# Neighbourhood values as float32 products, two heads side by side, and modulation weights in their own ring

## The chip, the cores and the metric

The kernel runs on one core of one Trainium2 chip. The metric is the device time of one execution in microseconds (us); lower is better.

## The reference

One step of a small transformer with two layers, on 512 latent tokens (a grid of 8 rows by 64 columns) and 128 prompt tokens, model width 1024, all in float32. Layer 0 mixes tokens by neighbourhood attention with 16 heads of 64; layer 1 by grouped-query attention with rotary positions. Each layer ends in a gated feed-forward part with a width-3 convolution. Scales, shifts and gates of both layers come from small products of the conditioning vectors with `ada_w`. The change is in layer 0, whose mixer is:

```python
q, k, v = split(h @ w_qkv)                       # 16 heads of 64
s_lat = einsum('brqhd,brkwhd->bhrqkw', qg, kg) * scale     # 8 rows x 16 columns around each query
s_lat = where(col_ok, s_lat + bias, -inf)
s_ctx = einsum('brqhd,bchd->bhrqc', qg, k_ctx) * scale     # 128 cached keys
p = softmax(concat([s_lat, s_ctx]))
o = einsum(p_lat, vg) + einsum(p_ctx, v_ctx)     # the value products
```

The prompt tokens attend only to each other. A modulation is `silu(c) @ ada_w + ada_b`, cut into six rows of 1024 for each layer.

## The kernel before

Tokens are 640 columns: 512 latent, 128 prompt. The NA stage (neighbourhood attention of layer 0, `with l_na`, from line 714) works head by head. `TensorE` follows an order written out by hand: every matmul depends on the one before it in program order (`pe`, line 97). The other engines' instructions stand in an order that a scheduler made when the kernel was built, and each engine takes them in that order.

**Splits.** Large products are made of float32r parts: a weight `raw` is loaded into the ring `wr` of the pool `wp` (4 buffers), ACT casts it to `wh`, POOL or DVE subtracts to get `wl` (`wsplit`, line 150), and three matmuls (high by high, low by high, high by low) go into one accumulation (`passes`, line 166).

**A head.** For each of 16 heads, `Head.scores(slot)` (line 874) makes the scores of one of four blocks of 128 queries: two matmuls `s`, a DVE step that adds the bias and takes the extreme, the exponential on ACT (`p`), a reciprocal on DVE, a multiplication on POOL. `Head.turns(i)` (line 894) transposes four 128x128 blocks of `p` into a PSUM bank `tp`, and `split_turned` (line 640) makes two parts of them: ACT casts to `th`, DVE subtracts to `tl`. `Head.values(i)` (line 903) multiplies both with the values. The value tile `vt` holds for each head 64 high columns and 64 low columns side by side, so that one matmul with 128 weight columns gives both halves: rows 0 to 63 of the bank `po` hold the high part, rows 64 to 127 the low part. `Head.out` (line 919) copies the two halves on ACT into `ot` tiles, and after the odd head of a pair `pair_out` (line 925) adds them on POOL into `of0`, which holds a pair of heads on 128 partitions. The prompt's attention (steps `p0`, `p1`, `p2`, once in four heads) does the same with `prompt_turn`, `prompt_out`.

**The order.** `ORDER` (line 46) is the list of a head's steps, and `ORDER2` that of heads 13 to 15. `t0` to `t2` are the transposes of this head, `s0` to `s3` the scores of the next, `v0` to `v2` the value products, `p0` to `p2` the prompt's. `f` takes the next step of `stream` (line 951), which runs through the query, key and value projections of later heads (`qk` and `vp`, 8 matmul groups each; their weights are loaded one item ahead), and after head 12 the first output products `y`. `a` takes the next step of `ada_work` (line 246), the modulation rows: a row of `ada_w` (128x1024) is loaded into `wr` of `wp`, and some steps later four matmuls `ada` of 32 weight columns use it as their moving operand. So projection weights and modulation weights take turns in one ring of four buffers (line 968).

**After head 12** the output weights are split (`m0.weights`, pinned in program order), `of0` is split into `oh` and `ol` (`o_split`, line 931), and the output products start.

Of the kernel before, what the change touches and what calls it, by code (L numbers as in the profile page):

```python
# [18 lines left out]
P = 128  # L19
D = 1024  # L20
KC = D // P
NS = 512
# [16 lines left out]
NPT = 6  # L39
TH = 322  # L40
# [5 lines left out]
ORDER = "a f a f p0 t0 a s0 f s1 t1 a f v0 t2 a a f a v1 f p1 f a a s2 a s3 v2 f f f a a p2 f f".split()  # L46
ORDER2 = "t0 p0 s0 s1 f a f a f f t1 v0 t2 a a f a f f a a p1 v1 s2 a f a s3 f v2 f p2 a f f".split()
# [44 lines left out]
def hybrid_step(ctx: ExitStack, tc: tile.TileContext, A, O):  # L92
# [330 lines left out]
    def na_v_tiles():  # L423
        return [vpool.tile([P, 6, 2, 2, HD], F32R, tag="vt", name="vt") for _ in range(2)]

    def na_v_put(vts, c, src):
        s4 = src.rearrange("p (a d) -> p a d", a=4)
        for i, vt in enumerate(vts):
            hi = vt[:, c, :, 0, :]
            nc.scalar.copy(hi, s4[:, 2 * i : 2 * i + 2, :])  # L430
            nc.vector.tensor_sub(vt[:, c, :, 1, :], s4[:, 2 * i : 2 * i + 2, :], f32(hi))
# [16 lines left out]
    with ExitStack() as s:  # L448
# [107 lines left out]
        vts_of[0] = na_v_tiles()  # L556
# [83 lines left out]
    def split_turned(ap, tp, n=512, nb=2):  # L640
        th = ap.tile([P, 512], F32R, tag="th", name="th", bufs=nb)
        tl = ap.tile([P, 512], F32R, tag="tl", name="tl", bufs=nb)
        nc.scalar.copy(th[:, 0:n], tp[:, 0:n])
        nc.vector.tensor_sub(tl[:, 0:n], tp[:, 0:n], f32(th[:, 0:n]))
        bk.put(tp)
        return th, tl

    def prompt_turn(ap, pp, nb=2):
# [3 lines left out]
        return split_turned(ap, tp, nb=nb)  # L652

    def prompt_out(ap, po, dsts):

        ta = ap.tile([P, 2, P], F32, tag="ta", name="ta", bufs=1)
        tb = ap.tile([P, 2, P], F32, tag="tb2", name="tb2", bufs=1)
        p4 = po.rearrange("p (a b c) -> p a b c", a=2, b=2)
        for b in range(2):
            own, _ = own_oth(b)  # L660
            nc.scalar.copy(ta[own], p4[0:64, :, b, :])
            nc.scalar.copy(tb[own], p4[64:128, :, b, :])
        bk.put(po)
        for j, dst in enumerate(dsts):
            nc.gpsimd.tensor_add(dst, ta[:, j, :], tb[:, j, :])
# [48 lines left out]
    with l_na:  # L714
# [12 lines left out]
        def na_v_items(g):  # L727
            d = {}

            def load():  # L730
                d["w"] = [wsplit(rows(wqkv, 4 * i, 4, 2048 + 256 * g, 256), 4, 256, nc.gpsimd) for i in range(2)]
                d["v"] = na_v_tiles()
# [122 lines left out]
        class Head:  # L855
# [38 lines left out]
            def turns(self, i):  # L894
# [6 lines left out]
                self.t[i] = split_turned(ap, tp)  # L901

            def values(self, i):
                b = self.b
                vt = vts_of[self.h // 4][(self.h // 2) % 2]
                if i == 0:
                    self.po = bk.get("po")
                po = self.po
                if i == 0:
                    for n, x in enumerate(self.t[i]):  # L910
                        mm(po, vt[:, 5, b, :, :], x, start=n == 0, stop=False)
                    return
                for a, c in enumerate(self.BANKS[i]):
                    ov = po[:, c * P : c * P + 256] if c < 3 else po.rearrange("p (a b) -> p a b", b=P)[:, 0::3, :]
                    for n, x in enumerate(self.t[i]):
                        mm(ov, vt[:, c, b, :, :], x[:, a * 256 : a * 256 + 256], start=False,
                           stop=c == 3 and n == 1)

            def out(self, tabs):
                own, _ = own_oth(self.b)  # L920
                nc.scalar.copy(tabs[0][own], self.po[0:64, :])
                nc.scalar.copy(tabs[1][own], self.po[64:128, :])
                bk.put(self.po)

        def pair_out(p, tabs):
            om = of0[p][:, 0:NS].rearrange("p (r c) -> p r c", c=GW)
# [41 lines left out]
        ada0 = ada_work(l_na.enter_context(pool("ada")), wp, 3, 2, ((0, 2), (0, 4), (0, 3)))  # L968
# [13 lines left out]
        tabs = None  # L982
        for h in range(H):
            nxt = Head(h + 1) if h + 1 < H else None
            if h % 2 == 0:
                tabs = [ap.tile([P, 512], F32, tag=f"ot{i}", name=f"ot{i}", bufs=1) for i in range(2)]
            g = h // 4
            pr = h % 4 == 1
            order = ORDER if h < 13 else ORDER2
            for i, step in enumerate(order):  # L990
# [9 lines left out]
                elif step[0] == "v":  # L1000
                    head.values(int(step[1]))
                if step == "v2":
                    head.out(tabs)
                    if h % 2:
                        pair_out(h // 2, tabs)
# [7 lines left out]
                if pr and step == "p1":  # L1013
                    pth = prompt_turn(ap, pp)
                if pr and step == "p2":
                    po = bk.get("po")
                    for j in range(4):
                        vt = vts_of[g][j // 2]
                        for n, x in enumerate(pth):
                            mm(po[:, j * P : j * P + P], vt[:, 4, j % 2, :, :], x[:, j * P : j * P + P],  # L1020
                               start=n == 0, stop=n == 1)
                    prompt_out(ap, po, [of0[2 * g + j][:, NS:T] for j in range(2)])
# [512 lines left out]
    def gqa_prompt(g):  # L1535
# [11 lines left out]
        def two():  # L1547
            tp = bk.get("tp")
            for i in range(4):
                turn(tp[:, i * P : i * P + P], d["pp"][:, i, :], ident)  # L1550
            x = d["t"] = d["pool"].tile([P, 4, P], F32, tag="ptp", name="ptp", bufs=1)
            nc.scalar.copy(x, tp.rearrange("p (a b) -> p a b", a=4))
            bk.put(tp)
# [270 lines left out]
```

## Time and profile before

| what | us |
|---|---|
| median of three runs (lowest to highest) | 1701.52 (1698.48 to 1703.72) |
| the profiled execution | 1699.22 |
| its span in the trace | 1697.4 |
| NA stage: heads 0 to 12, and the rest to the output products | 95 to 334, 334 to 395 |
| TensorE busy in the span | 94% |
| DVE, ACT, POOL busy in the span | 61%, 53%, 44% |

A row of the trace reads: start, duration, engine, line of the kernel, operation, tile written <- tiles read, shape. PE is TensorE's matmul, PEld its weight load, DVE VectorE, ACT ScalarE, POOL GpSimd; SPq is the queue of SyncE, which issues the large loads. A matmul's duration holds its way through the array, so that what it costs in a sequence is read from the start of the next one. The granted clock is the share of TensorE's clock that it was given.

### The profile page before, as it was taken

The numbers are of one execution on the slowest core, as the hardware profiler recorded it, in microseconds if no ns is written. First come the engines' busy times: TensorE is split into PE (matmuls) and PEld (weight loads), VectorE is DVE, ScalarE is ACT, GpSimd is POOL, SyncE is SP. The second block draws the span as 40 slices with busy tenths as digits, with TensorE's granted clock in tenths as the row PEclk, the third lists the DMA queues.
The fourth block names the chain that finished last, engine by engine and source line by source line (L and its number), as shares of the span: only waits on it lengthen the run. The fifth ranks groups of instructions, "written<-read, shape, count | busy, mean of one in ns | idle before, by whom it ended". The sixth has DMA issues, their size and how long they took to land.

```text
span 1697.4 us, 26300 instructions
## 1 busy us (share of the span) xinstructions
PE 1589.7 (94%) x9709; PEld 1376.1 (81%) x9709; DVE 1039.7 (61%) x1725; ACT 903.6 (53%) x1721; POOL 751.7 (44%) x651
## 2 busy tenths in 40 slices
PE   6899998999999899989979888999998999998998
PEld 3788897977988788988868666777887999997876
DVE  4444454557875555672375776775696788784264
ACT  5466657655554444553355444664555665663353
POOL 3544545444245354442344345442424555652253
PEclk9999999989999999999989998999999999999999
DMA  9544544116376576347557410001636333336574
GB/s 269 150 112 121 141 127 118 32 63 224 113 235 203 189 218 185 121 153 236 161 187 232 133 38 13 2 1 63 211 112 188 115 120 98 117 117 212 174 238 170
DMA packets 193220, 242.43 MB, mean 143 GB/s; under 512 B 11108, under 2 KB 149572, under 8 KB 193092
## 3 DMA queue, kind: packets, MB, share of 16 engines
q1 hardware_dynamic: 182232, 233.13, 43.7%
q10 hardware_dynamic: 10860, 7.62, 2.3%
q8 instruction: 76, 1.25, 0.3%
q14 instruction: 52, 0.43, 0.1%
HBM read 214.38 MB, written 26.34 MB: 142 GB/s over the span
## 4 chain that ended last, share of the span: by engine, by line
PE 58%; DVE 13%; DMA 8%; POOL 7%; ACT 6%; issue 6%; ACTq 1%; SPq 0%; POOLq 0%; DVEq 0%
PE acc L104 17%; PE ux L104 10%; PE y L104 5%; PE uz L104 4%; PE po L104 3%; PE s L104 3%; DMA wr<-in_ada_w 3%; PE tp L107 3%; PE qk L104 3%; PE uy L104 3%; PE vp L104 3%; DMA wr<-in_na_w_qkv 2%; POOL wl L1117 2%; DVE t L1193 2%; PE ada L104 2%
## 5 line engine op out<-in xcount | busy, mean ns | idle before, releaser
L157 POOL TENSOR_TENSOR wl<-wr,wh 128x1024 fp32r<-128x1024 f32 x80 | 196.3, 2457 | 279.6 <-ACT wh L155 274.9
L1117 POOL TENSOR_TENSOR wl<-wr,wh 128x1024 fp32r<-128x1024 f32 x80 | 194.7, 2451 | 68.7 <-ACT wh L1116 59.3
L104 PE MATMUL ux<-B,wh 128*128 128x322 f32 x832 | 201.9, 313 | 1.9 <-DVE B L210 1.8
L1193 DVE SCALAR_TENSOR_TENSOR t<-C,cw,t 128x644 f32<-128x644 f32 x176 | 156.6, 890 | 55.8 <-ACT t L1191 54.9
L104 PE MATMUL acc<-wh,alo 128*128 128x512 f32 x440 | 175.5, 399 | 10.7 <-DVE alo L1086 10.7
L104 PE MATMUL acc<-wh,ahi 128*128 128x512 f32 x440 | 175.6, 399 | 9.5 <-DVE act L1204 9.5
L155 ACT CAST wh<-wr 128x1024 fp32r<-128x1024 f32 x148 | 153.5, 1047 | 45.0 <-DMA wr<-in_na_w_qkv 17.5
L104 PE MATMUL acc<-wl,ahi 128*128 128x512 f32 x440 | 174.7, 397 | 0.0
L104 PE MATMUL uz<-B,wh 128*128 128x322 f32 x640 | 158.4, 315 | 0.0
L104 PEld LDWEIGHTS ux<-B,wh 128*128 128x128 f32 x832 | 143.6, 189 | 9.6 <-issue 3.3
L1086 DVE TENSOR_TENSOR alo<-ain,ahi 128x384 fp32r<-128x384 f32 (+1 forms) x88 | 55.1, 631 | 141.8 <-ACT ahi L1084 141.8
L104 PE MATMUL ux<-B,wl 128*128 128x322 f32 x416 | 129.2, 311 | 0.0
L1084 ACT CAST ahi<-ain 128x384 fp32r<-128x384 f32 (+1 forms) x88 | 40.5, 462 | 166.3 <-PE acc L104 139.8
L104 PE MATMUL qk<-hT,wh 128*128 128x384 f32 (+1 forms) x512 | 126.6, 320 | 0.4 <-DVE qs L799 0.4
L104 PEld LDWEIGHTS uz<-B,wh 128*128 128x128 f32 x640 | 111.6, 190 | 6.6 <-issue 3.7
L1117 POOL TENSOR_TENSOR vl<-wr,vh 128x1024 fp32r<-128x1024 f32 x38 | 96.5, 2540 | 34.2 <-ACT vh L1116 34.2
L104 PEld LDWEIGHTS acc<-wh,alo 128*128 128x128 f32 x440 | 84.4, 192 | 30.4 <-DVE alo L1086 11.9
L1116 ACT CAST wh<-wr 128x1024 fp32r<-128x1024 f32 x88 | 89.5, 1049 | 35.0 <-DVE wr L1140 33.6
L104 PEld LDWEIGHTS acc<-wh,ahi 128*128 128x128 f32 x440 | 84.6, 192 | 28.4 <-issue 10.2
L1191 ACT ACTIVATE t<-C,cw 128x644 f32<-128x644 f32 x88 | 78.7, 894 | 50.7 <-DVE C L1221 47.4
L157 DVE TENSOR_TENSOR wl<-wr,wh 128x1024 fp32r<-128x1024 f32 x68 | 91.1, 1353 | 21.5 <-ACT wh L155 21.0
L104 PE MATMUL uz<-B,wl 128*128 128x322 f32 x320 | 100.0, 313 | 0.5 <-POOL wl L1117 0.4
(264 smaller groups left out, 4193.8 us busy)
## 6 DMA issues: line engine op xcount, KB each, us to landing
wr<-in_ada_w SPq DMA_DIRECT2D x88, 512.0 KB
wr<-in_ffn_w_up SPq DMA_DIRECT2D x88, 512.0 KB
wr<-in_ffn_w_down SPq DMA_DIRECT2D x88, 512.0 KB
act<-act SPq DMA_DIRECT2D x44, 321.0 KB
wr<-in_na_w_qkv SPq DMA_DIRECT2D x24, 512.0 KB
mod<-modrow SPq DMA_DIRECT2D x20, 512.0 KB
ain<-act SPq DMA_DIRECT2D x44, 192.0 KB
xres<-xo SPq DMA_DIRECT2D x15, 512.0 KB
```

Source lines behind the costliest of these rows:

```text
L104: pe(nc.tensor.matmul(*a, **k))
L107: pe(nc.tensor.transpose(*a, **k))
L155: i = nc.scalar.copy(hi, raw)
L157: j = (low or nc.vector).tensor_sub(lo, raw, f32(hi))
L1084: nc.scalar.copy(hi[:, 0 : c1 - c0], ain[:, 0 : c1 - c0])
L1086: nc.vector.tensor_sub(lo[:, 0 : c1 - c0], ain[:, 0 : c1 - c0], f32(hi[:, 0 : c1 - c0]))
L1116: nc.scalar.copy(hl[0], src)
L1117: low.tensor_sub(hl[1], src, f32(hl[0]))
L1191: nc.scalar.activation(t, taps(0), AF.Identity, bias=cw[:, 3, n : n + 1], scale=cw[:, 1, n : n + 1])
L1193: nc.vector.scalar_tensor_tensor(t, taps(d), cw[:, w, n : n + 1], t, op0=ALU.mult, op1=ALU.add)
```

## The change

The value products are taken in plain float32. `vt` is now one float32 tile for a group of four heads with 64 columns a head, made by one ACT copy; there is no low part. `turns` copies the transposed block once, `t0` on ACT, `t1` and `t2` on DVE, into a ring `pk` of six buffers. The products wait until both heads of a pair have their transposes; then `values` issues for each block of keys two matmuls, one for each head, with 64 weight columns each: the even head writes partitions 0 to 63 of `po`, the odd head 64 to 127. Three ACT copies bring the bank straight into `of0`. `Head.out`, `pair_out`, `prompt_out` and `split_turned` go. The step lists become one for even and one for odd heads: the even head has 14 `f` (15 in `ORDER2`) and no `v`, the odd head 10 and one `v`; both lists had 12. The modulation rows get a ring `adar` of two buffers.

```diff
+NPK = 6
+NAR = 2
-ORDER = "a f a f p0 t0 a s0 f s1 t1 a f v0 t2 a a f a v1 f p1 f a a s2 a s3 v2 f f f a a p2 f f".split()
+ORDER = (
+    "a f a f t0 a s0 f s1 t1 a f f t2 a a f a f f a a s2 a s3 f f f a a f f f".split(),
+    "a f a f p0 t0 a s0 f s1 t1 a f t2 a a f a f f a a v s2 a s3 p1 f f a a f p2".split(),
+)
...
+    def na_v_tile():
+        return vpool.tile([P, 6, 4, HD], F32, tag="vt", name="vt", bufs=2)
+
+    def na_v_put(vt, c, src):
+        nc.scalar.copy(vt[:, c], src.rearrange("p (a d) -> p a d", a=4))
...
-                self.t[i] = split_turned(ap, tp)
+                x = self.t[i] = ap.tile([P, 512], F32, tag="pk", name="pk", bufs=NPK)
+                if i:
+                    nc.vector.tensor_copy(x, tp)
+                else:
+                    nc.scalar.copy(x, tp)
+                bk.put(tp)
+
+        def values(two):
+
+            po = bk.get("po")
+            vt = vts_of[two[0].h // 4]
+
+            def block(ov, c, x):
+                for v in two:
+                    rows_ = slice(64 * v.b, 64 * v.b + 64)
+                    mm(ov[rows_], vt[:, c, v.h % 4, :], x(v), start=c == 5, stop=c == 3)
+
+            block(po, 5, lambda v: v.t[0])
+            for i in (1, 2):
+                for a, c in enumerate(Head.BANKS[i]):
...
+                    block(ov, c, lambda v: v.t[i][:, a * 256 : a * 256 + 256])
+            om = of0[two[0].h // 2][:, 0:NS].rearrange("p (r c) -> p r c", c=GW)
             for c0, c1, q0 in ((8, 56, 128), (56, 64, 0), (0, 8, 64)):
-                v = [x[:, q0 : q0 + 8 * (c1 - c0)].rearrange("p (c r) -> p c r", r=8) for x in tabs]
-                nc.gpsimd.tensor_add(om[:, :, c0:c1].rearrange("p r c -> p c r"), v[0], v[1])
+                nc.scalar.copy(om[:, :, c0:c1].rearrange("p r c -> p c r"),
+                               po[:, q0 : q0 + 8 * (c1 - c0)].rearrange("p (c r) -> p c r", r=8))
+            bk.put(po)
...
-        ada0 = ada_work(l_na.enter_context(pool("ada")), wp, 3, 2, ((0, 2), (0, 4), (0, 3)))
+        ada0 = ada_work(
+            l_na.enter_context(pool("ada")), l_na.enter_context(pool("adar", NAR)), 3, 2, ((0, 2), (0, 4), (0, 3))
+        )
...
+                    for j in range(2):
+                        for b in range(2):
+                            mm(po[64 * b : 64 * b + 64, j * P : j * P + P], vts_of[g][:, 4, 2 * j + b, :],
+                               pth[:, 2 * j + b, :], start=True, stop=True)
```

TensorE's rows at the value step of head 1, before: the scores of the next head (`s`), the last four of this head's value matmuls (`po`, from the parts `th` and `tl`), and the projection that follows.

```order
L104 MATMUL s<-kh_1115,qs_931 128x384
L104 MATMUL s<-kl_713,qs_931 128x384
L104 MATMUL po<-th,vt 128x256
L104 MATMUL po<-tl,vt 128x256
L104 MATMUL po<-th,vt 128x2x128
L104 MATMUL po<-tl,vt 128x2x128
L104 MATMUL qk<-hT_127,wh 128x256
```

The same place now (`tk` is the transpose of a cached key block, `pp` the prompt's weights):

```order
L115 MATMUL tk<-ident,kc 128x128
L112 MATMUL po<-pk,vt 64x512 x2
L112 MATMUL po<-pk,vt 64x256 x6
L112 MATMUL po<-pk,vt 64x2x128 x2
L112 MATMUL s<-kh_1079,qs_915 128x384
L112 MATMUL s<-kl_694,qs_915 128x384
```

All ten value matmuls of heads 0 and 1 stand together, ahead of the scores; before, each head had ten of its own, spread over three places.

The queue of SyncE at the start of the stage, before. `in_na_w_qkv` are projection weights, `in_ada_w` modulation rows, `abias` and `again` small rows; all of the `wr` are one ring of four.

```order
L153 DMA wr<-in_na_w_qkv 128x8x128 x4
L267 DMA wr<-in_ada_w 128x1024 x3
L259 DMA abias<-in_ada_b 4x256
L261 DMA again<-in_norm_mix_post 4x256
L259 DMA abias<-in_ada_b 4x256
L261 DMA again<-in_norm_mix_post 4x256
L153 DMA wr<-in_na_w_qkv 128x8x128
L267 DMA wr<-in_ada_w 128x1024 x2
L153 DMA wr<-in_na_w_qkv 128x8x128
L267 DMA wr<-in_ada_w 128x1024
```

The same place now, where the `wr` of `in_ada_w` is the ring of two:

```order
L161 DMA wr<-in_na_w_qkv 128x8x128 x4
L275 DMA wr<-in_ada_w 128x1024 x2
L161 DMA wr<-in_na_w_qkv 128x8x128 x2
L161 DMA wr<-in_na_w_qkv 128x4x256
L267 DMA abias<-in_ada_b 4x256
L269 DMA again<-in_norm_mix_post 4x256
L267 DMA abias<-in_ada_b 4x256
L269 DMA again<-in_norm_mix_post 4x256
L161 DMA wr<-in_na_w_qkv 128x4x256
L161 DMA wr<-in_na_w_qkv 128x8x128 x2
L275 DMA wr<-in_ada_w 128x1024
```

Ten loads of projection weights stand ahead of the third modulation row now, where four stood ahead of it before.

ACT's rows at the end of head 1, before (`p` the exponentials, `ot` the two halves of `po`, `kh` parts of later keys), and behind them now:

```order
L888 ACTIVATE p,su<-s,nm 128x384 x2
L921 COPY ot_1012<-po 64x512
L922 COPY ot_1013<-po 64x512
L771 CAST kh_1444<-tk 64x128
L772 CAST kh_1444<-tk 64x128
```

```order
L758 CAST kh_1355<-qk 64x256
L911 COPY of_116<-po 128x48x8
L911 COPY of_116<-po 128x8x8 x2
L874 ACTIVATE p,su<-s,nm 128x384 x2
L649 COPY ptp<-tp 128x512
```

The output copies go straight into `of0` and stand ahead of the next head's exponentials instead of behind them.

More of the change, by code (lines that the diff above doesn't have):

```diff
@@ L638, in prompt_scores, with prompt_turn @@
         return pp
[L640 to L648, printed above, removed]
+    def prompt_turn(ap, pp, tag, nb):
         tp = bk.get("tp")
@@ L651, in prompt_turn @@
             turn(tp[:, i * P : i * P + P], pp[:, i, :], ident)
[L652 to L665, printed above, removed]
+        x = ap.tile([P, 512], F32, tag=tag, name="ptp", bufs=nb)
+        nc.scalar.copy(x, tp)
+        bk.put(tp)
+        return x.rearrange("p (a b) -> p a b", a=4)
     class Mix:
@@ L919, in out @@
[L919 to L926, printed above, removed]
+                x = self.t[i] = ap.tile([P, 512], F32, tag="pk", name="pk", bufs=NPK)
+                if i:
+                    nc.vector.tensor_copy(x, tp)
+                else:
+                    nc.scalar.copy(x, tp)
@@ L999, in hybrid_step @@
                     head.turns(int(step[1]))
[L1000 to L1005, printed above, removed]
+                elif step == "v":
+                    values((before, head))
                 if pr and step == "p0":
@@ L1547, in two @@
         def two():
[L1548 to L1553, printed above, removed]
+            d["t"] = prompt_turn(d["pool"], d["pp"], "ptp", 1)
         def three():
```

49 lines of the change are left out of this document (13 added, 36 removed).

## The prediction

> **What bounds the kernel now.** The page comes first, then the stretches of the neighbourhood stage, then who waited for whom on TensorE in them, and last the chain of waits at its longest pauses. Times are us; the first row is the span, the others are one row per stretch: length, then busy time of PE, PEld, DVE, ACT, POOL, and the granted clock.
>
> ```profile
> span 1697.4 us, 26300 instructions
> 95.00:334.00 239.00, 228.87 (x1668) 207.95 (x1668) 117.01 (x337) 152.37 (x401) 120.79 (x138) 0.97 0.41 112
> 334.00:357.00 23.00, 16.36 (x53) 10.91 (x52) 16.40 (x26) 16.48 (x37) 15.49 (x11) 0.63 0.27 94
> 357.00:395.00 38.00, 37.58 (x196) 31.26 (x195) 15.49 (x31) 21.03 (x45) 12.86 (x21) 1.00 0.31 109
> ```
>
> The change lies in these 300 us and TensorE bounds them: it is idle 10.1 us of the first 239, 6.6 of the next 23, 0.4 of the last 38. DVE, ACT and POOL have 40% to 60% to spare, so work taken from them counts only where TensorE waits for it. Its waits in the first stretch (line that waited, engine and line waited for, total, times, longest):
>
> ```profile
> PE po L104 <- DVE qs L799: 3.1, 1, 3.1
> PE sp L104 <- ACT kh L772: 2.5, 2, 1.3
> PE s L104 <- DVE qs L799: 1.9, 1, 1.9
> PE po L104 <- DVE kl L773: 0.8, 1, 0.8
> PE po L104 <- DVE tl L644: 0.7, 2, 0.5
> PE sp L104 <- DVE kl L773: 0.5, 2, 0.3
> ```
>
> These are 9.5 of the 10.1. None is arithmetic on DVE or ACT that takes so long: the producers came late. The chain says why, at the two longest (start, duration, what):
>
> ```profile
> 190.09 0.61 PE ada L104 x8
> 190.72 5.26 DMA wr<-in_na_w_qkv
> ...
> 197.13 2.38 POOL wl L157
> ```
>
> ```profile
> 251.00 4.92 DMA wr<-in_na_w_qkv
> ...
> 255.95 1.04 ACT wh L155
> ...
> 257.55 0.80 PE po L104
> ```
>
> In the first, a modulation product (`ada`) ends, only then does its buffer of the ring `wr` come free, and only then does a projection weight start to load. In the second the weight lands at 255.9; ACT, which works in order, casts it and only then reaches `qs`, which the `po` matmul's neighbours need. The view of the DMA queue's own waits and ACT's row in the view of all waits put sizes to it:
>
> ```profile
> SPq L153 <- PE ada L104: 46.1, 12, 6.0
> ACT wh L155 <- DMA wr<-in_na_w_qkv: 17.5, 10, 3.6
> ```
>
> A pause also costs afterwards. Each pair of rows is a window of 3.41 us and the next one (PE busy, ..., granted clock):
>
> ```profile
> 195.66:199.07 3.41, 1.55 (x11) 1.23 (x10) 1.10 (x4) 3.02 (x11) 1.94 (x1) 1.00 0.06 17
> 199.07:202.48 3.41, 3.41 (x13) 2.86 (x11) 2.19 (x7) 2.00 (x6) 3.37 (x5) 0.50 0.50 150
> 253.69:257.10 3.41, 0.78 (x7) 0.54 (x5) 1.14 (x3) 1.12 (x2) 0.88 (x2) 1.00 0.40 115
> 257.10:260.51 3.41, 2.96 (x14) 1.58 (x14) 1.75 (x6) 3.31 (x11) 3.41 (x3) 0.50 0.07 11
> ```
>
> A window with PE busy for 1.55 or 0.78 is followed by one at half clock, which loses up to 3.41 x 0.5 = 1.7. Over the first stretch the clock is 0.97: 0.03 x 239 = 7.2 us lost, about four such windows.
>
> **Part 1: the value products, on the path.** Before, a head takes 2 matmuls of 512 columns and 8 of 256, twelve units of 256. After, a pair of heads takes one block of 512 and four of 256, six units, each unit two float32 instructions side by side. The nearest float32 row is the later grouped-query stage, which has this form already; first the old form, then the new one:
>
> ```profile
> 112.68 0.28 PE L104 MATMUL po<-th,vt 128*128 128x256 f32 x1
> ...
> 113.15 0.34 PE L104 MATMUL qk<-hT,wh 128*128 128x384 f32 x1
> ```
>
> ```profile
> L104 PE MATMUL po<-pk,gvt x320: 379/379/430, 1059.0 to 1192.6; 128*64 128x256 f32 x160
> ```
>
> ```profile
> 1190.04 0.39 PE L104 MATMUL y<-wl,ph 128*128 128x512 f32 x1
> 1190.27 0.39 PE L104 MATMUL y<-wh,pl 128*128 128x512 f32 x1
> 1190.59 2.38 PE L104 MATMUL po<-pk,gvt 128*64 128x256 f32 x20
> 1192.90 0.50 PE L104 MATMUL y<-wh,ph 128*128 128x512 f32 x1
> ```
>
> Four old matmuls take 113.15 - 112.68 = 0.47, so a head takes 12 x 0.1175 = 1.41 and a pair 2.82. In the new form the code issues 160 matmuls in that stage and the trace holds 320 records: a float32 matmul leaves two, one for each of its passes. So the x20 is ten instructions, five units for two heads, and takes 1192.90 - 1190.59 = 2.31, plus 0.32 - 0.23 = 0.09 more than the usual spacing ahead of it. That is 0.48 a unit, and six units take at most 2.88. With the ends of a group counted once instead of in proportion I take 2.85. Eight pairs: 8 x 0.03 = **+0.2**, between -1.5 (without ends) and +0.5. [...]
>
> The trace has that toll at the ends, 0.09 ahead of the group and about as much behind it. The Trainium skill, TensorEngine Tiling (Array Packing), Key Properties, says that changing the tiling mode drains the engine; the old 128x128 values changed nothing, so by that rule this change pays where it did not before. The trace agrees, and the 0.2 a group is within the 2.85; without the rule the term would be -1.5 instead of +0.2.
>
> The prompt's four groups change likewise (first and next row of the old form):
>
> ```profile
> 137.66 0.33 PE L104 MATMUL po<-th,vt 128*128 128x128 f32 x1
> ...
> 138.61 0.39 PE L104 MATMUL qk<-hT,wh 128*128 128x384 f32 x1
> ```
>
> 0.95 before; after, two units of 128 columns, half of 0.44 each, and 0.2 at the ends: 0.64. Four times: **-1.2**, between -1.8 and 0.
>
> **Part 2: less for ACT, DVE and POOL, beside the path.** Rows: count, min/median/max ns.
>
> ```profile
> L643 ACT CAST th<-tp x52: 573/587/619, 104.2 to 381.5; 128x512 fp32r<-128x512 f32 x52
> L644 DVE TENSOR_TENSOR tl<-tp,th x52: 659/691/693, 105.3 to 382.1; 128x512 fp32r<-128x512 f32 x52
> L921 ACT COPY ot<-po x16: 566/578/582, 114.6 to 383.9; 64x512 f32<-64x512 f32 x16
> L1667 DVE COPY pk<-tp x48: 406/673/692, 1055.1 to 1181.5; 128x512 f32<-128x512 f32 x32, 128x256 f32<-128x256 f32 x16
> ```
>
> DVE loses 52 x 0.69 = 36 us and gets 32 x 0.68 = 22 back. ACT loses 52 x 0.59 = 31 and 32 output copies of 0.58 = 19; it keeps 20 casts' worth of copies (12) and three strided output copies a pair. The trace has no strided ACT copy out of PSUM; between the 0.58 of a whole 512-column copy for all three and 1.7 for three such, I take 1.0, so 8. ACT is about 30 us lighter, DVE 14 (more with the low parts of `vt`), POOL loses its additions. On its own this is worth nothing while TensorE is busy; it shortens the queues that its waits stand in, and `po` no longer waits for `tl` (0.7) with nothing between.
>
> **Part 3: the ring of their own.** The projection weights keep all four `wr` buffers, so the chain `ada`, DMA, cast at 190 can't occur, and a weight loads up to four loads ahead of its cast instead of behind three modulation rows. The waits on `qs`, `kh` and `kl` above are 8.8. I count **-8** of the 10.1 (between 0 and -10), and of the 7.2 lost to half clock **-5.5** (0 to -7), since three or four of the windows go with their pauses. What is late next: the pause ahead of 95, where the first pair's keys are awaited, which no edit touches, and the stretch 334 to 357. There POOL sets the pace:
>
> ```profile
> 340.59 10.54 POOL L157 TENSOR_TENSOR wl<-wr,wh 128x1024 fp32r<-128x1024 f32 x4 [3.55 <-ACT wh L155]
> ```
>
> These four splits are pinned behind head 12 in both versions, and the output projection waits for them. The two `ot` copies and POOL's additions ahead of them go, the fewer steps of odd heads leave less to fill with: **-0.5** (-1.5 to +1.5).
>
> Sum: +0.2 - 1.2 - 8 - 5.5 - 0.5 = -15.0. The profiled execution took 1699.2 (span 1697.4 and 1.8 around it): 1684.2. The median of the three runs before lies 2.3 above that execution, so **1686.5**.
>
> **Rivals.** *The half clock stays* (0.10): waits go, half-rate windows come at other pauses. -9.5: 1692. For it speaks the Trainium skill, TensorE: Matmul & The Clock Gate, What's actually happening: half rate follows an idle window of about 3.4 us, which would not tie it to waits of 2 us. The trace differs: the window ahead of 199.07 had TensorE busy 1.55, and the next was at half.
>
> *Half of it comes back* (0.17): even heads now have 14 projection steps and odd heads 10, ACT and DVE get a new order, and new waits of some 0.5 us arise at `pk`, `kh` or `s`. -7: 1694.5. For it: six of the eight kinds of wait above stand behind such queues; against: both engines are lighter.
>
> *Nothing to measure* (0.12): as many new waits as old ones. About 1700.
>
> *Slower* (0.06): the modulation ring has two buffers. If its loads land late, TensorE itself stops at `ada`, since it works in order, with everything behind it. First the ring of four shared in this stage, then the ring of two in the feed-forward stage:
>
> ```profile
> L104 PE MATMUL ada<-wr,scolp x192: 379/403/637, 100.5 to 281.4; 128*32 128x256 f32 x192
>   DMA wr<-in_ada_w: 0.4, 2
> ```
>
> ```profile
>   DMA wr<-in_ada_w: 23.0, 13
> ```
>
> There 48 loads lost 23.0 in 13 waits; for 24 loads that is 11.5, and six or seven half-clock windows of 1.7 are 11 more: 1686.5 + 22.5 = 1709. Against it: 24 loads in 281.4 - 100.5 = 181 us are 7.9 apart, so two buffers leave 15.7 from a buffer's release to its next use, and a load takes 5. It decides where the queue holds a load back for over 10.
>
> *The halves do not run side by side* (0.02): each unit doubles, 6 x 0.44 x 8 = +21: 1707. Against it stands the x20 row. *More* (0.03): the other 2 of idle, 1.7 of clock and the 6.6 idle of 334 to 357 go as well: about 1674.
>
> **How the numbers follow.** The forecast, 1680 to 1690, has 0.50. Faster by over 0.3% (5.1 us, about what a measurement of this kernel can tell from no change) hold the forecast, the first two rivals and "more": 0.80; within 0.3%: 0.12; slower: 0.08. The range reaches from nearly full recovery, 1675, to 1700, where nothing is recovered but the prompt's term; outside it lie the two slower rivals and part of the third, under 0.2.
>
> **What would show it.** Right: idle of TensorE in the stage from 95 to the end of head 12 falls from 10 to 2, clock there 0.99, no wait of ACT `wh` for its DMA, a pair's `po` group about 2.85 long with 20 records or more, 334 to 357 unchanged in length. Wrong: `ada` waiting for DMA, `po` groups near 5, or idle of 6 or more with `kh`, `pk` or `s` as the ones waited for.

## The result and the profile after

The changed kernel takes 1677.65 us (median of 4 runs, 1675.57 to 1679.24), the kernel before 1700.0 (4 runs beside it, 1695.11 to 1703.72). The ratio is 0.9869, with a 95% interval from 0.9846 to 0.9892: **faster**, by 1.1% to 1.5%. That is clear of the spread between runs, though it is less than 2%, the mark under which a difference is counted as "same" in this record; of the kernels below only the two with a ratio under 0.98 pass that mark. The forecast was 1686.5 with a range from 1675 to 1700. The time lies inside the range, 9 us below the likeliest value and 2 below the band from 1680 to 1690 that had half of the chances. The profiled execution after took 1675.57, with a span of 1673.7.

The first row is the page's span. Then come the windows that answer to those of before, in the same columns: length, busy time of PE, PEld, DVE, ACT, POOL, granted clock. The first pair of heads starts and head 12 ends earlier now, so the stretches have moved.

```profile
span 1673.7 us, 26080 instructions
92.50:311.50 219.00, 218.57 (x1656) 192.03 (x1655) 94.77 (x283) 122.95 (x344) 107.19 (x114) 1.00 0.44 117
311.50:334.50 23.00, 16.46 (x55) 11.48 (x55) 15.84 (x25) 14.13 (x33) 15.47 (x11) 0.63 0.29 95
334.50:373.00 38.50, 38.50 (x207) 29.95 (x204) 13.87 (x28) 16.16 (x39) 10.33 (x15) 1.00 0.31 106
```

Idle time of TensorE in the first stretch is 219.00 - 218.57 = 0.4, where it was 10.1, and the clock there is 1.00 instead of 0.97. The second window was laid as long as the one of before; idle time in it (6.5 and 6.6) and clock (0.63) are the same.

To see where the 23.7 us of span went, take five places on TensorE in both traces: the first score matmul `s`, the first output projection `y`, the first matmul `ux` of the feed-forward part, the first `acc` behind it, and the end.

| part | before | after | difference |
|---|---|---|---|
| start to first `s` | 93.1 | 90.4 | -2.7 |
| heads: first `s` to first `y` | 249.0 | 229.2 | **-19.8** |
| output projection, to first `ux` | 79.8 | 78.9 | -0.9 |
| feed-forward, to first `acc` | 334.0 | 338.6 | +4.6 |
| the rest | 941.5 | 936.6 | -4.9 |

The two rows of the heads, before and after, in the columns of the windows:

```profile
93.10:342.10 249.00, 235.78 (x1696) 213.63 (x1696) 121.92 (x349) 161.12 (x419) 125.09 (x143) 0.96 0.39 107
```

```profile
90.40:319.60 229.20, 225.29 (x1686) 197.56 (x1686) 100.27 (x299) 132.95 (x363) 114.41 (x120) 0.99 0.43 114
```

DVE is 21.7 lighter, ACT 28.2, POOL 10.7, all of it beside the path. TensorE's idle time falls from 13.2 to 3.9; its busy time falls by 10.5 with 10 instructions fewer, since a matmul at half clock counts as busy for longer (in this trace one `s` of 384 columns follows another after 0.32 to 0.43 at half clock, after 0.17 to 0.18 at full clock). Of the 19.8, idle time is 9.3 and the clock about 7.7 (0.04 x 249.0 - 0.01 x 229.2); about 1 is the prompt's products, and the other 2 are no more than a clock of two digits leaves open. In what follows "the heads" is this row; one row of it per kernel is the measure that the experiments are read by. It comes from a single execution: the two profiles that have the stage of before as it was give 249.0 and 251.8.

The waits of TensorE from 85 to 380 after (line that waited, engine and line waited for, total, times, longest):

```profile
PE y L112 <- DVE ol L918: 3.3, 3, 1.3
PE tp L115 <- POOL p L878: 2.7, 2, 2.5
PE s L112 <- ACT kh L758: 1.4, 1, 1.4
PE y L112 <- ACT oh L917: 0.5, 1, 0.5
PE s L112 <- DVE kl L759: 0.2, 1, 0.2
PE qk L112 <- DVE qs L785: 0.2, 1, 0.2
```

Of the waits of 9.5 inside the stage before, 0.2 is left, the last row. The two rows of `s` are the wait ahead of the first scores; the waits at `y` belong to the stretch in which POOL splits the projection weights. One is new: `tp` waits 2.7 for POOL, 2.5 of it at 312, with the following rows on POOL (start, length, what, idle time ahead of it and what ended it).

```profile
312.79 1.66 POOL L835 TENSOR_TENSOR tb<-mask,tr 128x256 f32<-128x256 f32 x2 [3.69 <-DVE nm L870]
314.43 1.14 POOL L878 TENSOR_SCALAR p<-p,rc 128x384 f32<-128x384 f32 x2
316.14 10.52 POOL L165 TENSOR_TENSOR wl<-wr,wh 128x1024 fp32r<-128x1024 f32 x4 [0.58 <-ACT wh L163]
```

The second stretch begins with it, and its 10.52 of splits are the 10.54 of before.

The value products after, on TensorE (start, length, what); the x20 are a pair of heads:

```profile
124.44 0.27 PE L115 MATMUL tk<-ident,kc 128*128 128x128 f32 x1
124.64 2.81 PE L112 MATMUL po<-pk,vt 128*64 128x512 f32 x20
127.38 0.44 PE L112 MATMUL s<-kh,qs 128*128 128x384 f32 x1
```

```profile
132.63 0.66 PE L112 MATMUL po<-ptp,vt 128*64 128x128 f32 x8
133.22 0.44 PE L112 MATMUL qk<-hT,wh 128*128 128x384 f32 x1
```

From the group's start to the next row it is 2.74 for a pair and 0.59 for the prompt. And the queue of SyncE, in the view of the DMA queue's own waits from 92 to 320:

```profile
SPq L161 <- POOL wl L165: 128.8, 18, 30.8
SPq L275 <- PE ada L112: 64.4, 16, 7.7
```

SyncE still waits for `ada`, 64.4 in all. Before it was 84.6: the 46.1 of the prediction at the loads of projection weights, and 38.5 at those of modulation rows. Now all of it is at L275, a modulation load that waits for its own ring, and none at a projection weight's load. The weights are further ahead: L161 waits 128.8 for POOL to finish with them, up to 30.8 at a time, where L153 waited 33.9 before, up to 10.9. There is no wait of ACT's `wh` for its DMA left, where it was 17.5.

### The profile page after: what moved, and what is told of

The parts are those of the page before. It is cut to its first block, busy times and chain, and to the rows that moved or that the text cites. A ratio compares the mean times of both kernels' runs of the same rounds, so it can differ in the third digit from the quotient of the medians.

```text
span 1673.7 us, 26080 instructions
## 1 busy us (share of the span) xinstructions
PE 1575.5 (94%) x9709; PEld 1356.7 (81%) x9709; DVE 1014.7 (61%) x1657; ACT 867.1 (52%) x1649; POOL 735.6 (44%) x619
## 4 chain that ended last, share of the span: by engine, by line
PE 44%; DVE 13%; POOL 6%; issue 5%; DMA 4%; ACT 3%; SPq 0%; ACTq 0%; POOLq 0%; DVEq 0%
PE acc L112 17%; PE ux L112 9%; PE uz L112 4%; PE y L112 3%; PE uy L112 2%; PE s L112 2%; PE po L112 2%; DMA wr<-in_ada_w 2%; DVE t L1174 2%; POOL wl L1098 2%; PE tp L115 2%; DVE al L1098 1%; PE ada L112 1%; POOL vl L1098 1%; POOL rh L1409 1%
## 5 line engine op out<-in xcount | busy, mean ns | idle before, releaser
L112 PE MATMUL acc<-wh,alo 128*128 128x512 f32 x440 | 175.4, 399 | 10.7 <-DVE alo L1067 10.7
L112 PEld LDWEIGHTS acc<-wh,ahi 128*128 128x128 f32 x440 | 84.6, 192 | 28.3 <-issue 10.0
```

Of the source, the lines that this page charges most:

```text
L112: pe(nc.tensor.matmul(*a, **k))
```

## The experiments

**Theory:** most of the gain is the ring of its own, since it unties the weights' loads from `ada`; the pauses and the half-clock windows behind them were late weights. **Rivals:** the value products by themselves (side by side halves, or less work for ACT, DVE and POOL); the new step lists, which are a by-product (14 steps for even heads, 10 for odd); the feed-forward part, which gave back some of the gain. Each kernel was compared with the kernel before on the same chip. They are named here by what they change; two columns give the heads' and the feed-forward part's length in the profiled execution.

| kernel | median us | runs | ratio to before [95%] | heads | feed-forward |
|---|---|---|---|---|---|
| changed | 1677.65 | 4 | 0.9869 [0.9846, 0.9892] | 229.2 | 338.6 |
| shared ring | 1689.13 | 6 | 0.9930 [0.9905, 0.9955] | 238.8 | 335.6 |
| halves apart | 1693.72 | 10 | 0.9962 [0.9948, 0.9976] | 239.8 | 338.7 |
| lists alike | 1672.05 | 6 | 0.9848 [0.9821, 0.9874] | 227.4 | 330.3 |
| heavy copies | 1677.43 | 4 | 0.9873 [0.9851, 0.9895] | 229.4 | 336.0 |
| before, no rows loaded | 1680.34 | 6 | 0.9896 [0.9878, 0.9915] | 234.7 | 332.1 |
| changed, no rows loaded | 1675.13 | 5 | 0.9840 [0.9817, 0.9863] | 229.1 | 336.0 |
| ring of one | 1687.92 | 6 | 0.9934 [0.9914, 0.9954] | 240.4 | 334.4 |
| splits between | 1680.16 | 5 | 0.9891 [0.9872, 0.9910] | 228.2 | 340.0 |
| feed-forward ring of three | 1660.22 | 4 | 0.9778 [0.9758, 0.9798] | 229.2 | 322.2 |
| before, feed-forward ring of three | 1683.74 | 6 | 0.9896 [0.9875, 0.9916] | 251.8 | 321.1 |
| lists alike, feed-forward ring of three | 1660.08 | 4 | 0.9752 [0.9730, 0.9774] | 228.9 | 322.1 |

### The modulation rows back in the weights' ring

```diff
-            l_na.enter_context(pool("ada")), l_na.enter_context(pool("adar", NAR)), 3, 2, ((0, 2), (0, 4), (0, 3))
+        ada0 = ada_work(l_na.enter_context(pool("ada")), wp, 3, 2, ((0, 2), (0, 4), (0, 3)))
```

> The changed kernel with one thing undone: the modulation rows of the neighbourhood stage load into the ring of four that the projection weights use, as before. Theory A (late weight loads behind modulation rows made the pauses): TensorE's waits on qs, kh or kl come back behind ACT casts that wait for a weight's load, some 5 to 10 us of idle and two to four half-clock windows between 92 and 312, so 1686 to 1695 where the changed kernel takes 1678 and the one before 1700. Rival B (the lighter ACT and DVE queues, and the new step lists, did it): under 4 us of idle, 1677 to 1682.

Measured: 0.993, so 11.5 us of the gain are gone (1689.13 - 1677.65), and the heads take 238.8. The chain of waits, at 116 to 124 and at 242 to 249 (start, length, what):

```profile
115.70 2.40 POOL wl L165
118.10 0.02 issue
118.11 3.57 DMA wr<-in_na_w_qkv
...
122.77 0.39 ACT qs L784
...
123.18 0.44 DVE qs L785
...
123.75 0.59 PE s L112 x2
```

```profile
242.22 0.61 PE ada L112 x8
...
242.85 5.67 DMA wr<-in_na_w_qkv
...
248.55 1.04 ACT wh L163
```

In both a weight lands late, ACT casts it, and only then reaches `qs`. The second has the shape of the prediction's first chain, with `ada` ahead of the load. In the first it is POOL's `wl` that frees the buffer. The waits on TensorE, and those of ACT and of the queue:

```profile
PE s L112 <- DVE qs L785: 3.2, 1, 3.2
PE vp L112 <- DVE kl L759: 2.7, 1, 2.7
...
PE qk L112 <- DVE qs L785: 1.6, 1, 1.6
```

```profile
ACT wh L163 <- DMA wr<-in_na_w_qkv: 15.9, 12, 3.3
```

```profile
SPq L161 <- PE ada L112: 55.5, 12, 10.8
```

The three pauses are 7.5, ACT waits 15.9 for weights as it did 17.5 before, and the queue's wait behind `ada` stands at the weights' load again. With all of the value path as in the change, the ring alone brings pauses back. Two of the three, 4.8, end the chains above. The chain of the other, 2.7, goes back through ACT to a load of the bias table (`tr`, 5.38 us) and not to a weight; how the shared ring brings that one about is not shown. The two to four half-clock windows that were expected did not come in this execution, the fastest of the six (1680.16; the others took 1684.06 to 1692.27): its clock is 1.00 in every window of 3.41 us from 95.2 to 320.5.

### The kernel before without the modulation loads, and the changed kernel without them

```diff
-                    raw = rawp.tile([P, D], F32, tag="wr", name="wr")
-                    nc.sync.dma_start(raw, A["ada_w"][l, k * P : k * P + P, idx * D : idx * D + D])
+                    raw = None
+                    if load:
+                        raw = rawp.tile([P, D], F32, tag="wr", name="wr")
+                        nc.sync.dma_start(raw, A["ada_w"][l, k * P : k * P + P, idx * D : idx * D + D])
...
-                        mm(ps[32 * j : 32 * j + 32, 0:256], scolp[:, 2 * kk : 2 * kk + 32], raw[:, 256 * j : 256 * j + 256],
+                        mm(ps[32 * j : 32 * j + 32, 0:256], scolp[:, 2 * kk : 2 * kk + 32],
+                           raw[:, 256 * j : 256 * j + 256] if load else bias,
```

The neighbourhood stage calls it with `load` false, the feed-forward stage as ever. Without the rows neither kernel makes the three modulation rows of the reference. First in the kernel before:

> The kernel before, with the modulation rows of the neighbourhood stage taken out of the shared ring by leaving their 24 loads out: the same ada matmuls read a small tile that lies in SBUF anyway, so the three modulation rows that they make are not those of the reference. Value products, splits and step lists are those of before. Theory A (half of the gain or more is the ring): no ACT cast waits for a projection weight, waits on qs, kh and kl of 8.8 us fall under 3, 1686 to 1692 against 1700. Rival B (what made the difference is the new value path and order alone): 1697 or more.

Then in the changed kernel:

> The changed kernel with the 24 modulation rows of the neighbourhood stage left out (the ada matmuls read a small tile in SBUF, so three modulation rows are not those of the reference), as in the run of the kernel before without these rows: no ring question in either, so the two differ by the value products and the step lists alone. If these are worth something of their own: heads from the first s to the first y in 227 to 231 us where the kernel before without rows took 234.7, and 3 to 6 us of the time. If they only matter through the ring: 233 to 236. If a ring of two still costs something, this is also below the 229.2 of the changed kernel.

The heads' row of each:

```profile
91.60:326.30 234.70, 230.04 (x1696) 209.66 (x1696) 119.25 (x349) 159.86 (x419) 124.76 (x143) 0.98 0.27 61
```

```profile
90.70:319.91 229.21, 225.22 (x1685) 197.50 (x1685) 100.34 (x299) 132.89 (x364) 114.37 (x120) 0.99 0.28 64
```

Without the loads the old value path needs 234.7, 14.3 less than before. The time, 1680.34, is below the 1686 to 1692 expected; what goes beyond the 14.3 lies in parts with the same code, most of it behind the stage. TensorE's waits there, in the first of these two kernels:

```profile
PE s L104 <- ACT kh L775: 2.4, 1, 2.4
PE tk L107 <- ACT kp L816: 1.6, 1, 1.6
PE po L104 <- DVE qs L802: 0.7, 2, 0.5
PE sp L104 <- DVE kl L776: 0.6, 2, 0.3
PE sp L104 <- ACT kh L775: 0.4, 1, 0.4
PE qk L104 <- DVE qs L802: 0.4, 1, 0.4
```

The first row stands ahead of the first scores. The waits for `qs`, `kl` and `kh` behind it are 2.1, where the prediction counted 8.8. So without the loads, and with them the coupling, 14.3 of the 19.8 are there with the old value path. The new value path without the loads needs 229.1 (from its first `s` at 90.77; the row above starts a little earlier), and with them 229.2: a ring of two costs nothing here, although 24 loads of 512 KB more pass through the queue. Between the two rows lies the worth of the value path with its lists: 5.5, of which 0.7 is idle time (4.7 against 4.0) and 4.8 busy time, at a clock of 0.98 and 0.99. In the times of the two kernels it is 5.2 (1680.34 and 1675.13), as expected, and by their ratios, each taken beside its own runs of the kernel before, 0.0056 of 1700, 9.5.

Taken in the other order, from the change with a shared ring, the value path and the lists bring 249.0 - 238.8 = 10.2 and the ring then 9.6. If the two rows without loads stand for the ring, the two parts overlap by 4.7. With a spread of 2.8 between profiles the size of this is uncertain. A reason could be that lighter engines catch up sooner behind a late weight; no run tests that.

No run gives the kernel before a modulation ring of its own, and none gives both streams one ring of six. So it is not tested directly whether the separation counts or the two buffers that came with it. The ring of one, below, speaks for the separation: with one buffer more than before, no cast waits for a projection weight.

### The two heads one after the other

```diff
-            def block(ov, c, x):
-                for v in two:
+            def block(ov, c, x, who):
+                for v in who:
...
+            for w in two:
+                block(po, 5, lambda v: v.t[0], (w,))
```

> The changed kernel with the value matmuls of a pair issued head after head: five of the even head, then five of the odd one, so that no two neighbours in the order use different halves of the columns. Same products, same number. If a unit of 256 columns costs the same 0.44 us for one head as for two side by side, a pair's group goes from 2.74 to about 5.3 us, eight pairs cost 8 x 2.6 = 21 us more, and the time is 1695 to 1700, all of the gain. If the engine overlaps halves also over five matmuls, the group stays under 3.5 us and the time under 1684.

```profile
124.71 4.58 PE L112 MATMUL po<-pk,vt 128*64 128x512 f32 x20
129.22 0.44 PE L112 MATMUL s<-kh,qs 128*128 128x384 f32 x1
```

4.51 to the next row, against 2.74: the same twenty records take 1.77 longer when the two halves of the columns do not alternate. Six of the eight groups lie in the heads' row: 6 x 1.77 = 10.6, and the row grew by 239.8 - 229.2 = 10.6. That the two agree to the tenth is luck, since idle time is 1.5 longer than in the changed kernel and the clock 1.00 instead of 0.99. The whole kernel grew by 16.1, of which 8 x 1.77 = 14.2 are accounted for. The time, 1693.72, lies between the two forecasts, near the first. The order of ten instructions is thus worth at least as much as the ring. The group is not doubled, to 12 x 0.44 = 5.3: in the records the odd head's first 512-column matmul (at 126.49 and 126.97) runs beside the even head's last four (starts at 126.48 to 127.13, 0.22 apart), and this seam, 126.49 to 127.35, is long enough for the 0.8 that is missing.

### ACT and DVE made heavy again

```diff
-                if i:
-                    nc.vector.tensor_copy(x, tp)
-                else:
-                    nc.scalar.copy(x, tp)
+                nc.scalar.copy(x, tp)
+                nc.vector.tensor_sub(tp, tp, x)
```

ACT makes all three copies as it made the casts, and DVE subtracts as before; the difference goes to nobody.

> The changed kernel with ACT and DVE as busy behind the transposes as before: ACT makes all three copies of a head, and DVE subtracts each copy from the bank (a result that nothing uses) before the bank comes free. 32 more ACT copies of 0.58 us and 48 DVE subtractions of 0.69 in place of 32 copies of 0.67: ACT 19 us and DVE 12 us heavier in 230. Theory A: TensorE still has its weights in time, 1677 to 1683. Rival B (lighter queues made the gain): waits on kh, kl or pk of over 5 us, 1684 to 1692.

0.9873 against 0.9869, and the heads take 229.4: no change, with ACT 146.6 busy there instead of 133.0 and DVE 107.8 instead of 100.3. With a ring of its own for the modulation rows, the lighter copies at the transposes are worth nothing.

### The step lists alike

```diff
-    "a f a f t0 a s0 f s1 t1 a f f t2 a a f a f f a a s2 a s3 f f f a a f f f".split(),
-    "a f a f p0 t0 a s0 f s1 t1 a f t2 a a f a f f a a v s2 a s3 p1 f f a a f p2".split(),
+    "a f a f t0 a s0 f s1 t1 a f t2 a a f a f f a a s2 a s3 f f f a a f f".split(),
+    "a f a f p0 t0 a s0 f s1 t1 a f t2 a a f a f f a a v s2 a s3 p1 f f f a a p2 f f".split(),
```

The two lists of the last heads likewise (13 and 12): twelve projection steps for each head instead of 14 and 10.

> The changed kernel with the same number of projection steps in even and odd heads (12 and 12, in the last three heads 12 to 13) instead of 14 and 10. Theory A: the lists only balance TensorE's work between heads; within 3 us of the changed kernel, 1675 to 1681. Rival C (the two more projection steps ahead of a new pair's first scores are what removed the waits of s and sp): waits of s or sp on kh and qs of 4 us or more come back, 1682 to 1690.

The time, 1672.05, is under both forecasts. The ratio, 0.9848, is below the change's, but the intervals overlap, and the heads' row, 227.4, is only 1.8 shorter; 8.3 are in the feed-forward part, whose code is the same. In the stage itself the new wait of `tp` for POOL is all but gone, 0.3 instead of 2.7, so it came with the lists of 14 and 10:

```profile
PE tp L115 <- POOL p L878: 0.3, 1, 0.3
```

To take the feed-forward part out of the comparison, both were run with a feed-forward ring that does not wait (next).

### The same question in the feed-forward part

There the modulation rows have a ring of two already, and `ada` waits for its DMA. One buffer more, in the changed kernel, in the kernel before, and with the lists alike:

```diff
-                ada = ada_work(adap, s2.enter_context(pool("adar", 2, side)), 1, 1, todo)
+                ada = ada_work(adap, s2.enter_context(pool("adar", 3, side)), 1, 1, todo)
```

> The changed kernel with three buffers instead of two in the modulation ring of the first feed-forward part (not the one of this change). There TensorE waits 13.1 us for modulation rows in the changed kernel's trace, 10.6 in that of before, and the part took 338.6 us against 334.0. If the ring's length is the cause, these waits fall under 4 and the time to 1664 to 1670. If the queue of SyncE holds the rows back behind other loads, the waits stay over 9 and the time is 1675 to 1680.

> The kernel before with three buffers instead of two in the modulation ring of the first feed-forward part, nothing else. Theory A (the change gains about 20 us in the neighbourhood stage and gives some back in the feed-forward part, where its trace has 13.1 us of waits for modulation rows and 338.6 us in place of 334.0): the feed-forward part takes 322, the time 1685 to 1690, so that the changed kernel with the same three buffers (1660) is 25 to 30 better, more than the 22 of the pair with two. Rival D (the feed-forward part has no share in it): the gain is the same here, 1678 to 1684, and the pair differs by 18 to 22.

> The changed kernel with both: step lists of 12 and 12, and three buffers in the modulation ring of the first feed-forward part. If the lists alike were faster (1672 against 1678) because of the feed-forward part, where that run waited 7.4 us for modulation rows instead of 13.1, the two gains are the same one: 1657 to 1661, as with three buffers alone (1660). If the lists gain in the neighbourhood stage, where a wait of 2.5 us ahead of y went, both add up: 1652 to 1656.

The wait of `ada` from 395 to 760, in the changed kernel with two buffers and with three:

```profile
PE ada L112 <- DMA wr<-in_ada_w: 13.1, 6, 5.6
```

```profile
PE ada L112 <- DMA wr<-in_ada_w: 1.1, 1, 1.1
```

The wait goes, the part takes 322.2 instead of 338.6, and the kernel 1660.22 us, less than either forecast: 0.9778 of the kernel before. In the kernel before, one buffer more brings the part to 321.1, the same. With a ring that does not wait, the change is worth 0.9778 / 0.9896 = 0.988, which is the ratio that it had with two buffers, 0.987, to within the intervals. In the times the pair differs by 23.5, between the two forecasts (18 to 22 and 25 to 30), but it was not run beside the same runs of before; by the ratios it is 0.0118 of 1700, 20.1, and 1683.74 lies within Rival D's range. So the +4.6 in the table of parts does not show a cost of the change: the same code with two buffers took 330.3 to 340.0 in the nine profiles of the table that have it and in that of before. And the lists alike lose their advantage: 1660.08 against 1660.22. They are worth nothing that these times can tell.

### A ring of one

```diff
-NAR = 2
+NAR = 1
```

> The changed kernel with one buffer in the modulation ring instead of two. A row's load can start only when the products of the row before are done, 7.9 us ahead of its own use, and takes about 5. The forecast's reading (a load is late only where the queue holds it back by more than the slack) gives a slack of about 3 us: a few waits of ada for its DMA, 2 to 10 us in all, 1679 to 1690. If two buffers were already at the edge, waits in most of the 24 places, over 20 us, 1700 and more. If loads never stand in the queue, no wait, 1676 to 1679.

```profile
PE ada L112 <- DMA wr<-in_ada_w: 7.0, 5, 3.5
```

```profile
89.64:330.11 240.47, 228.74 (x1686) 200.09 (x1686) 100.62 (x301) 133.02 (x364) 114.40 (x120) 0.97 0.42 110
```

The first row is TensorE's longest kind of wait up to the output projection, the second the heads. `ada` stops TensorE for 7.0 there, the clock falls to 0.97, close to the 0.96 of before, and the kernel loses 10.3. No cast of ACT waits for a projection weight, so the coupling is away with this ring too. The mechanism of the prediction's slower rival lies one buffer away, at less than half of the 22.5 that was put for it.

### POOL's splits spread over the last heads

```diff
-                for p in range(6):
-                    o_split(p)
+                    if u < 3:
+                        o_split(2 * u)
+                        o_split(2 * u + 1)
```

> The changed kernel with the splits behind head 12 in another order: after each output weight's split the two head pairs that it is multiplied with, instead of all four weights first. In the changed kernel y waits 3.8 us for oh and ol and the clock is at half for 17 us from 315.7. If ACT's four casts ahead of the first oh set the start of y, the first y comes some 2 to 3 us earlier and the time is 1672 to 1676. If POOL's four subtractions (2.5 us each, beside which ol takes up to 3 us) set the pace, nothing changes: 1676 to 1680.

0.9891, within the interval of the change; the time, 1680.16, is 0.2 above the second forecast, in which nothing changes. TensorE's wait at `y` for `ol` grew from 3.3 to 4.9, and POOL's four last splits still stand in one piece:

```profile
316.22 11.11 POOL L165 TENSOR_TENSOR wl<-wr,wh 128x1024 fp32r<-128x1024 f32 x4 [0.57 <-ACT wh L163]
```

They took 10.54 before and 10.52 after. TensorE's waits there are for `ol`, which DVE makes meanwhile (0.81 to 2.99 us apiece in the changed kernel). That POOL's splits set the pace of this stretch fits the three traces, but no run shortens them, so it is not shown.

## Why the prediction was right, and where it was off

**The direction and the mechanism were right**: waits of TensorE on late weights, tied to `ada` by a shared ring, and the half clock behind them. Point by point:

- *Value products, +0.2.* Measured 2.74 a pair, and 0.09 ahead of it (124.64 - 124.44 = 0.20 against the 0.11 to 0.12 of the rows ahead), 2.83 against 2.82: nothing. The Trainium skill, TensorEngine Tiling (Array Packing), Key Properties, says that a change of the tiling mode drains the engine; the trace agrees, with 0.09 ahead and 2.74 - 6 x 0.44 = 0.10 at the end of a group. The prediction took the two records of a float32 matmul for its passes; the trace shows that there are two, 0.22 apart at 256 columns, and not what they are.
- *Prompt, -1.2.* 0.95 before and 0.59 + 0.1 after, four times: -1.0.
- *Waits, -8.* This is the first **mis-sized term**: 9.7 of the 10.1 went. The prediction held back 2 for waits of a new order; the only new one is the 2.5 at `tp`, which came with the new lists, and it stands in the stretch behind.
- *Half clock, -5.5.* The second mis-sized term: all of the 7.2 went, since every half-clock window between 92 and 312 vanished with the pauses. Part of that is luck. The window that began at 93.3, behind the wait ahead of the first scores, comes back at 91.6 with the ring of one and at 91.2 with the lists alike and the ring of three, and costs up to 1.7 of the heads' row there.
- *The two chains.* The first, at 190, is told rightly. The second, at 251, does not begin with `ada`. POOL's additions of the two halves (`of`), and behind them its `wl`, kept the weight's buffer until 250.99:

```profile
247.05 1.57 POOL of L929 x3
248.62 2.37 POOL wl L157
251.00 4.92 DMA wr<-in_na_w_qkv
```

  So the longest pause, 3.1, hung on POOL too, and those additions are work that the new value path takes away. The prediction counted this pause as the ring's. Without the modulation loads, but with the additions, it went as well (0.7 of waits for `qs` ahead of `po` are left).
- *The stretch behind, -0.5.* In windows of the same 23 us idle time is 6.5 against 6.6 and the clock 0.63 both times: right to within half a microsecond.
- *"The pause ahead of 95 ... which no edit touches"* failed as put. The low part of the values is made ahead of the first keys, on the same engines, and with the edit that work is lighter; that this is the cause was not tested. TensorE's wait there was 2.4 to 2.5 in all three profiles with the old values and 1.4 to 1.8 in all with the new ones. The first `s` came 2.7 earlier; the starts of the two kinds lie at 91.6 to 93.1 and 89.5 to 92.7, so about 1 us of it is shown and the rest is within the spread.
- *Strided output copies, 1.0 a pair.* Measured (count, min/median/max ns, forms), they are 0.86 + 2 x 0.33 = 1.5; ACT has the room.

```profile
L911 ACT COPY of<-po x24: 319/336/862, 127.5 to 362.5; 128x64 f32<-128x64 f32 x16, 128x384 f32<-128x384 f32 x8
```

Against its own profiled execution the forecast was 1684.2, and 1675.6 came, 8.6 less. Of these, 5.3 are in the heads (19.8 where +0.2 - 1.2 - 8 - 5.5 = -14.5 was put; the two mis-sized terms are 3.4 of it, and the rest is no more than a clock read to two digits leaves open over 249 us), 2.7 ahead of the first scores, 0.4 in the output projection, and 0.3 in later parts with the same code, where +4.6 and -4.9 cancel by luck: the feed-forward part's spread is told above, and in the rest the 941.5 of before is the longest of all profiles, which otherwise take 935.5 to 939.3. That these parts did not move the sum is not to the prediction's credit.

The prediction gave the ring 13.5 and the value path 1, and did not see that they overlap. By the runs the modulation loads alone are 14.3, the value path then 5.5; the value path first is 10.2, the ring then 9.6. In the medians the ring is 11.5 of 22.3, so about half of the gain or more is the ring's. Without the side-by-side order the value path would cost 16 more. What makes the 5.5 is not split further: the copies at the transposes are not it, the prompt is 1.0 of it, and the value casts and output copies were not tried alone.

Of the rivals, "more" came nearest in its parts: the other 2 of idle time and 1.7 of clock went as it put them, the 6.6 of idle time behind the heads did not. "Half clock stays" fell in this pair of profiles. The shared-ring run leaves its rule open all the same. Two windows of it, around the 3.2 wait (length, busy time of PE, ..., clock):

```profile
119.11:122.52 3.41, 1.46 (x9) 1.14 (x7) 0.58 (x2) 0.82 (x1) 0.00 (x0) 1.00 0.87 306
122.52:125.93 3.41, 2.17 (x18) 2.17 (x19) 1.99 (x8) 3.36 (x14) 3.11 (x2) 1.00 0.01 4
```

TensorE was busy 1.46 of a window (1.62 of one laid 0.16 earlier, where this trace's changes of clock fall), and full clock followed. In the kernel before, the window from 120.60 had it busy for 1.86, and the next was at 0.50. The Trainium skill, TensorE: Matmul & The Clock Gate, What's actually happening, has half rate follow an idle window; none of these was idle throughout, and their busy time alone does not decide it either. What does stays open.

## What to carry to other kernels

When one ring of buffers serves two streams, an in-order queue makes the loads of the one wait for the consumer of the other: look at the queue's own waits for a load that waits on an engine which has nothing to do with it, and give each stream its ring. Count then the buffers of each: here one was 10 us too few, two were enough in one stage, and in the next stage a third was worth 17. A wait on a saturated engine costs its length and, where a half-clock window follows it, up to 1.7 us more.

## What the hardware showed that was not expected

- Float32 matmuls in opposite column halves overlap with their neighbour only: alternating, twenty records took 2.74; head after head 4.51, with the overlap at the one seam.
- The runs of one kernel can differ with the granted clock: the shared-ring kernel took 1680.16 at a clock of 0.982 over the whole span and 1691.15 at 0.974. A single profile per kernel is therefore read by stages that the change touches.
- ACT's copy of 128x384 out of PSUM, written with strides (48 blocks of 8), took 0.86 us, though the plain copy of more columns, 64x512, took 0.58 before.
